# A hybrid recurrence–attention block on eight cores: output projection and first layer norm woven into the next tile's projections, recurrence steps spread, row loads on another queue

## Chip, cores, metric

One Trainium2 chip, all 8 cores; each core works through 2 of the 16 sequences, and no core waits for another. The time of a run is that of the slowest core, in device microseconds (us). A run is *slow* when the four cores of one die are granted a lower TensorE clock than the others and end over 1% later, or when it is over 1.5% above the fastest of the same kernel. Only fast runs are compared, and within a slow run only the cores of the undisturbed die. Engines: PE = TensorE, PEld = its weight loads, DVE = VectorE, ACT = ScalarE, POOL = GpSimd, SP = SyncE.

## The reference, cut

```python
BATCH, SEQ, D_MODEL = 16, 4096, 1024      # D_FF = 2816
def reference(x, c, ...):
    mod = (silu(c) @ w_ada + b_ada)[:, None, :]
    sh1, sc1, g1, sh2, sc2, g2 = jnp.split(mod, 6, axis=-1)
    h = x * (1.0 + sc1) + sh1
    proj = h @ w_in
    aq, af, ai, ag, bq, bk, bv, bf, gates = jnp.split(proj, splits, axis=-1)
    ya = hgrn2_mixer(aq, af, ai, ag, ...)      # gated linear recurrence, 4 heads of 128, head norm, output gate ag
    yb = forgetting_attention(bq, bk, bv, bf)  # causal softmax attention with decay, 8 heads of 64
    gate_a, gate_b = jnp.split(sigmoid(gates), 2, axis=-1)
    merged = gate_a * (ya @ w_branch_a) + gate_b * (yb @ w_branch_b)
    x = layer_norm(ALPHA * x + (1.0 + g1) * (merged @ w_out), ln1_w, ln1_b)
    h = x * (1.0 + sc2) + sh2
    ffn = (silu(h @ w_ffn_gate) * (h @ w_ffn_up)) @ w_ffn_down
    return layer_norm(ALPHA * x + (1.0 + g2) * ffn, ln2_w, ln2_b)
```

## The kernel before

A tile is 512 tokens; a core has 16 of them. The loop over tiles has three stages: M(i) merges the branches of tile i, P(i+1) makes the projections and the recurrence of tile i+1, and F(i) (feed-forward) runs interleaved with A(i+1) (attention). Weights come from HBM in pieces of up to 1 MB through a ring of buffers, all requested on SP's queue in the order of use; `get_piece` waits for the next, `release` frees the oldest.

```python
def load_bc(slot, src, reads=()):                 # one row of norm or gate weights, to all partitions
    P.dma("sync", "bc%d" % slot, bc[:, slot, :], src.partition_broadcast(128), ...)

def ln_acc(s4, nh, b):                            # residual add, half a row block
    TT("vector", TMP[:, ti, :], ps[b], bc[:, 0, ...], mult, ...)
    STT(sl, sl, ALPHA, TMP[:, ti, :], mult, add, ...)
    bn_stats(st[:, s4, nh, :], sl)

def stage_P(i, hooks):                            # hooks: ln_norm(3), 8 transposes to h2T, 4 POOL affines
    # piece f: 4 groups of 8 matmuls -> tanh -> TMP[h]
    # piece i: 4 groups -> G[12+s4], and after each group chain(s4):
    def chain(h):                                 # decay of one head
        ACT(X, TMP[h], Ln); scan(Y <- X) on DVE; ACT(eb[h], Y, Exp); ACT(X, Y, Exp, scale=-1)
        TS("gpsimd", TMP[h] affine); TT("vector", G[4+h] <- TMP[h] * X); CP("vector", ebl[h] <- eb[h])
    # piece k: 4 groups, 2 hooks after each
    # piece q: 4 groups -> G[h] = ps * eb[h]; transposes of G[4+h]
    # piece v: 4 groups -> V1; one hook after each
    cstep(0); cnorm1(0)
    # piece Q: 4 groups; after groups 1, 2, 3: cstep(c), cnorm2(c-1), cnorm1(c)
    cnorm2(3)
    # piece g: 4 groups -> tanh (ACT) -> affine (POOL) -> ya = normed * gate (POOL)

    def cstep(c):                                 # one step of the recurrence
        # 16 matmuls 128x128: output from Sbf and from the chunk; state update
        TT("vector", TMP[3] <- ps[bD] + S); TT("vector", S <- TMP[3] * ebl); CP("scalar", Sbf <- S)

def gen_A(i):                                     # attention; the last row sums are exchanged and inverted at its end
    ...
    while pend: do_pv(*pend.pop(0))
    while ev: run_ev()

def stage_M(i):
    load_xT(i + 1)                                # 3 loads on SP's queue
    for nh in range(2):
        # gate a (4 groups of 8), branch a (4 of 4), branch b (4 of 4)
        if nh == 0:
            load_gate(i, 0); load_bc(1, lnv_d[0])             # rows; then x rows on POOL's queue
        # gate b: 4 groups -> tanh, STT, TT -> G[4*nh + dl]
    wos = [get_piece(), get_piece()]
    for s4 in range(4):                           # output projection: one block of 64 matmuls
        for nh in range(2):
            mmt8(b, wos[nh], lhs=G[0:8]); ln_acc(s4, nh, b)
        ln_rstd(s4)
        conv_hT(i + 1, 2 * s4); conv_hT(i + 1, 2 * s4 + 1)    # next tile's input: even ones on DVE, odd ones on ACT
        if s4 > 0: ln_norm(s4 - 1)
    release(2); load_bc(0, lnv_d[1])
```

Of the kernel before, what the change touches and what calls it, by code (L numbers as in the profile page):

```python
# [162 lines left out]
def build(NSEQ, SEQ):  # L163
    NT = SEQ // 512
    NKT = SEQ // 128
    NTI = NSEQ * NT
# [56 lines left out]
    bc = sb("bc", [128, 2, D], F32)  # L223
    rl = sb("rl", [128, 512], F32)
# [134 lines left out]
    def pieces_P():  # L359
        for j in (0, 2, 5, 1, 6, 4, 3):  # L360
            pieces.append((win_s[j], 4096, "win%d" % j))

    def pieces_M():
        for nh in range(2):
            pieces.append((win_s[7 + nh], 4096, "win%d" % (7 + nh)))
            pieces.append((wa_s[nh], 2048, "wa%d" % nh))
            pieces.append((wb_s[nh], 2048, "wb%d" % nh))
            pieces.append((win_s[9 + nh], 4096, "win%d" % (9 + nh)))
        for nh in range(2):
            pieces.append((wo_s[nh], 4096, "wo%d" % nh))  # L370
# [8 lines left out]
    pieces_P()  # L379
    for i in range(NTI):  # L380
        pieces_M()
        if i + 1 < NTI:
            pieces_P()
        pieces_F()
# [30 lines left out]
    for j in (0, 2, 5, 1, 6, 4, 3):  # L415
        conv_win(j)
# [77 lines left out]
    def conv_hT(i, kc):  # L494
        s = i // NT
        sc, sh = modT[:, s, 8 + kc:9 + kc], modT[:, s, kc:kc + 1]
        if kc % 2:
# [13 lines left out]
    def ln_acc(s4, nh, b):  # L511
        sl = xres[:, s4, nh * 512:(nh + 1) * 512]
        ti = (2 * s4 + nh) % 6
# [20 lines left out]
    def load_bc(slot, src, reads=()):  # L534
        P.dma("sync", "bc%d" % slot, bc[:, slot, :], src.partition_broadcast(128), reads=list(reads), writes=["bc%d" % slot])
# [6 lines left out]
    def stage_P(i, hooks):  # L542
# [3 lines left out]
        hooks = list(hooks)  # L546

        def hook(n=1):
            for _ in range(n):
                if hooks:  # L550
                    hooks.pop(0)()

        if t == 0:
            MSET("gpsimd", v2(S[:]), 0.0, ["S"])
            MSET("gpsimd", v2(Sbf[:]), 0.0, ["Sbf"])
            MSET("vector", CT[:, 0, :, :].rearrange("p a b -> p (a b)"), 0.0, ["CT"])

        XY = [(TMP[:, 4, :], TMP[:, 5, :], [Tk(4)], [Tk(5)]), (rl[:], cpO[:], ["rl0", "rl1", "rl2", "rl3"], ["cpOa", "cpOb"])]

        def chain(h):  # L560
            X, Y, XK, YK = XY[h % 2]
# [8 lines left out]


# [6 lines left out]
        release()  # L578
# [8 lines left out]
        release()  # L587

        pvr, pkey = get_piece()
        pv = v3(pvr, 8)  # L590
        for hp in range(4):
            b = rotD()
            mm8(b, pv, pkey, hp, HT, HTK)
            CP("scalar" if hp % 2 else "vector", KT[:, hp, tok0:tok0 + 512], ps[b][:, :], pk(b), ["KT%d_%d" % (t, hp)])
            hook(2)
# [13 lines left out]
        def s2(h):  # L609
            bb = (0, 1, 2, 3)[h]  # L610
# [6 lines left out]
        for h in range(4):  # L617
            b = rotD()
            mm8(b, pv, pkey, h, HT, HTK)
            TT("vector", G[:, h, :], ps[b][:, :], eb[h], ALU.mult, pk(b) + EBK[h], [Gk(h)])  # L620
            if h == 1:
# [5 lines left out]
        def cstep(c):  # L627
# [3 lines left out]
            for h in range(4):  # L631
                hs = slice(h * 128, (h + 1) * 128)
                MM(ps[bO][:, hs], Sbf[:, h, :], G[:, h, cs], True, False, ["Sbf", Gk(h)], pk(bO))
                MM(ps[bO][:, hs], G[:, 12 + c, hs], G[:, 16 + h, cs], False, True, [Gk(12 + c), Gk(16 + h)], pk(bO))
            for h in range(4):
                hs = slice(h * 128, (h + 1) * 128)
                MM(ps[bD][:, hs], G[:, 8 + h, cs], G[:, 12 + c, hs], True, True, [Gk(8 + h), Gk(12 + c)], pk(bD))
# [3 lines left out]
            CP("scalar", v2(Sbf[:]), v2(S[:]), ["S"], ["Sbf"])  # L641

        SQ = [(TMP[:, 4, :], [Tk(4)]), (TMP[:, 5, :], [Tk(5)]), (rl[:], ["rl0", "rl1", "rl2", "rl3"]), (cpO[:], ["cpOa", "cpOb"])]

        def cnorm1(c):
            sq, sqk = SQ[c]
            ACT(sq, ps[3 + c % 2][:, :], AF.Square, pk(3 + c % 2), sqk)

        def cnorm2(c):
            sq, sqk = SQ[c]  # L650
            bR = 2
# [3 lines left out]
            TT("vector", TMP[:, c, :], ps[3 + c % 2][:, :], sq, ALU.mult, pk(3 + c % 2) + sqk, [Tk(c)])  # L655
# [4 lines left out]
        for s4 in range(4):  # L660
# [4 lines left out]
            hook(1)  # L665
# [11 lines left out]
        cnorm1(0)  # L677
# [3 lines left out]
        for hp in range(4):  # L681
            b = rotD()
            mm8(b, pv, pkey, hp, HT, HTK)
            if hp % 2:
                ACT(Q[:, hp, :], ps[b][:, :], AF.Identity, pk(b), ["Q%d" % hp], scale=0.125)
            else:
                TS("vector", Q[:, hp, :], ps[b][:, :], 0.125, None, ALU.mult, None, pk(b), ["Q%d" % hp])
            if hp == 0:
# [10 lines left out]
            else:  # L699
                cstep(hp)  # L700
                cnorm2(hp - 1)
                cnorm1(hp)
            hook(1)
        release()
        cnorm2(3)
# [3 lines left out]
        for h in range(4):  # L709
            b = rotD()  # L710
            mm8(b, pv, pkey, h, HT, HTK)
            ACT(eb[h], ps[b][:, :], AF.Tanh, pk(b), EBK[h], scale=0.5)
            TS("gpsimd", eb[h], eb[h], nwT[:, h:h + 1], nwT[:, h:h + 1], ALU.mult, ALU.add, EBK[h] + ["nwT"], EBK[h])
            TT("gpsimd", ya[:, h, :].rearrange("p (a b) -> p a b", a=4), TMP[:, 0:4, h * 128:(h + 1) * 128],
               eb[h].rearrange("p (a b) -> p a b", a=4), ALU.mult, [Tk(0), Tk(1), Tk(2), Tk(3)] + EBK[h], ["ya%d" % h])
            hook(1)
        release()
        hook(len(hooks))
# [93 lines left out]
    def gen_F(i):  # L812
        for j in range(6):
# [4 lines left out]
            for fl in range(nfl):  # L818
                fc = 4 * j + fl
                ti = fc % 6  # L820
# [47 lines left out]
    def stage_M(i):  # L868
# [3 lines left out]
        for nh in range(2):  # L872
# [17 lines left out]
            pb_r, pb_k = get_piece()  # L890
            pb = v3(pb_r[:, 0:2048], 4)
            b2 = []
            for dl in range(4):
                b = rotM()
# [170 lines left out]
```

## Time and profile before

| | before |
|---|---|
| runs | 6266.2, 6285.6 (fast), 6594.1 (slow) |
| profiled run, cores | 6226.6 to 6265.6 us, clock 0.903 to 0.906 |
| PE busy, slowest core (core 1) | 4955.7 us of 6265.6 |
| one boundary: first gate matmul of M to first feed-forward matmul, mean of tiles 1 to 14, core 1 | 184.1 us, 52.1 idle |
| the 15 feed-forward-and-attention stages together | 2650.7 us, 72.7 idle |

The boundary between tiles is the place to look, as nine tenths of the idle time of the middle tiles lie there (14 x 52.1 = 730 us against 72.7). The prediction shows the lines.

### The profile page before, as it was taken

Reading aid. Unit: us, or ns where it says so; the run is one execution under the profiler, and the core shown is the slowest. Engines: PE = TensorE matmul, PEld = TensorE weight load, DVE = VectorE, ACT = ScalarE, POOL = GpSimd, SP = SyncE. Lnnn points to the kernel's source line nnn. Section 1 sums busy time; section 2 is a strip of 40 time slices with the busy share of each in tenths; the row PEclk is TensorE's granted clock in tenths of the full one; section 3 lists DMA queues with packets and bytes.
Section 4 is the critical chain, followed back from the end, with each engine's and each line's share of the span. In section 5 each row is a group of like instructions: output and inputs, shape, how many; then the busy total and the mean of one; then the engine's idle time right before and its main releaser. Section 6 shows DMA issues by size and latency. Waiting matters only on the chain.

```text
span 6265.6 us, 82655 instructions; the slowest of 8 cores (6226.6 to 6265.6 us)
## 1 busy us (share of the span) xinstructions
PE 4955.7 (79%) x26204; PEld 2019.3 (32%) x26204; DVE 2278.0 (36%) x3257; ACT 2396.2 (38%) x4034; POOL 1460.7 (23%) x1664
## 2 busy tenths in 40 slices
PE   3045796979889797987978687887979798897987
PEld 1011333323333333333333233333333333333333
DVE  0010434343434434334343434344443434334243
ACT  1011232424345363644722232433436263562741
POOL 0011213232222212222122323232231222213122
PEclk7577998989999898999989898999989899998998
DMA  8753334242423334242243425242332424224233
GB/s 169 106 91 104 128 110 157 103 163 90 165 94 120 125 103 150 84 147 91 90 150 110 163 91 176 96 167 87 133 125 103 156 91 157 87 96 140 89 140 108
DMA packets 231940, 759.90 MB, mean 121 GB/s; under 512 B 20017, under 2 KB 110685, under 8 KB 176223
## 3 DMA queue, kind: packets, MB, share of 16 engines
q1 hardware_dynamic: 165922, 637.66, 29.8%
q0 software_dynamic: 53312, 100.17, 6.8%
q10 hardware_dynamic: 12288, 16.79, 1.0%
q8 instruction: 226, 3.70, 0.2%
q14 instruction: 192, 1.57, 0.1%
HBM read 737.25 MB, written 66.60 MB: 128 GB/s over the span
## 4 chain that ended last, share of the span: by engine, by line
PE 59%; issue 10%; DVE 10%; POOL 7%; DMA 7%; ACT 5%; ACTq 1%; DVEq 0%; SPq 0%; POOLq 0%
PE ps L263 58%; POOL xres L277 4%; DMA ring<-win_s 3%; ACT TMP L274 2%; DVE TMP L277 2%; DMA rl<-cpL 2%; DVE rl L755 1%; DVE xres L286 1%; PE ps L266 1%; POOL ya L277 1%; DMA xres<-w_ada 1%; DVE st L516 1%; DVE TMP L286 1%; DVE S L277 1%; ACT PT L274 1%
## 5 line engine op out<-in xcount | busy, mean ns | idle before, releaser
L263 PE MATMUL ps<-hT,ring 128*128 128x512 bf16 x4608 | 1160.3, 411 | 599.1 <-DVE G L292 261.0
L274 ACT ACTIVATE PT<-ps,nb 128x512 bf16<-128x512 f32 (+3 forms) x2304 | 1311.5, 654 | 650.6 <-PE ps L263 644.1
L263 PE MATMUL ps<-h2T,ring 128*128 128x512 bf16 x5632 | 1320.1, 384 | 67.4 <-DVE TMP L286 60.7
L274 ACT ACTIVATE TMP<-ps 128x512 f32<-128x512 f32 (+1 forms) x760 | 445.5, 591 | 1416.5 <-PE ps L263 1361.3
L286 DVE SCALAR_TENSOR_TENSOR TMP<-TMP,ps 128x512 f32<-128x512 f32 x608 | 414.4, 686 | 1506.3 <-ACT TMP L274 1416.7
L263 PE MATMUL ps<-ring,G 128*128 128x512 bf16 x3840 | 878.5, 382 | 45.2 <-DVE G L277 40.0
L263 PEld LDWEIGHTS ps<-hT,ring 128*128 128x128 bf16 x4608 | 477.3, 105 | 1242.2 <-issue 816.0
L263 PEld LDWEIGHTS ps<-h2T,ring 128*128 128x128 bf16 x5632 | 514.5, 98 | 769.4 <-issue 231.9
L277 POOL TENSOR_TENSOR xres<-xres,bc 128x1024 f32<-128x1024 f32 x256 | 618.3, 2423 | 395.9 <-PE ps L266 369.3
L263 PEld LDWEIGHTS ps<-ring,G 128*128 128x128 bf16 x3840 | 359.5, 98 | 506.8 <-issue 108.4
L277 POOL TENSOR_TENSOR PT<-PT,Ub 128x128 bf16<-128x128 bf16 x512 | 210.1, 428 | 1319.1 <-ACT PT L274 1310.9
L274 ACT ACTIVATE xres<-xres,nmr,rstd 128x1024 f32<-128x1024 f32 x128 | 158.9, 1241 | 583.9 <-POOL nmr L283 537.3
L263 PE MATMUL ps<-PT,V 128*64 128x512 bf16 (+3 forms) x2304 | 344.0, 378 | 19.2 <-ACT cpO L290 17.7
L277 DVE TENSOR_TENSOR G<-TMP,ps 128x512 bf16<-128x512 f32 x352 | 241.7, 687 | 288.9 <-PE ps L263 276.3
L277 DVE TENSOR_TENSOR TMP<-ps,bc 128x512 f32<-128x512 f32 x256 | 174.5, 682 | 470.8 <-PE ps L263 470.8
L263 PE MATMUL ps<-Q,KT 64*128 64x512 bf16 (+3 forms) x2304 | 338.8, 367 | 3.7 <-ACT PT L274 1.9
L755 DVE RECIPROCAL rl<-rl 128x128 f32<-128x128 f32 x256 | 243.0, 949 | 231.1 <-POOL rl L277 213.6
L277 DVE TENSOR_TENSOR G<-TMP 128x512 bf16<-128x512 f32 x160 | 195.2, 1220 | 285.4 <-POOL TMP L283 230.0
L263 PE MATMUL ps<-ya,ring 128*128 128x512 bf16 x512 | 143.8, 437 | 115.5 <-DVE TMP L277 115.5
L522 POOL TENSOR_SCALAR rstd<-mv 128x1 f32<-128x1 f32 x128 | 35.6, 278 | 854.3 <-DVE mv L519 854.3
L263 PE MATMUL ps<-ring,hT 128*128 128x512 bf16 x1024 | 234.1, 379 | 0.0
L263 PE MATMUL ps<-PT,onesb 128*32 128x512 bf16 (+3 forms) x2304 | 224.8, 376 | 0.0
(132 smaller groups left out, 3541.8 us busy)
## 6 DMA issues: line engine op xcount, KB each, us to landing
ring<-win_s SPq DMA_DIRECT2D x176, 1024.0 KB, 6.1
ring<-wg_s SPq DMA_DIRECT2D x80, 1024.0 KB, 4.9
ring<-wu_s SPq DMA_DIRECT2D x80, 1024.0 KB, 4.9
ring<-wd_s SPq DMA_DIRECT2D x64, 1024.0 KB, 5.0
xres<-x POOLq DMA_DIRECT2D x64, 512.0 KB, 16.6
ring<-wo_s SPq DMA_DIRECT2D x32, 1024.0 KB, 16.9
y<-xres POOLq DMA_DIRECT2D x64, 512.0 KB, 3.7
xres<-w_ada SPq DMA_DIRECT2D x24, 1024.0 KB, 7.1
```

Source lines behind the costliest of these rows:

```text
L263: P.op("tensor", lambda e: e.matmul(out, lhsT=lhsT, rhs=rhs, start=start, stop=stop), r, w)
L266: P.op("tensor", lambda e: e.transpose(out=out, in_=in_, identity=ident), r, w)
L274: P.op("scalar", lambda e: e.activation(out=out, in_=in_, func=func, **kw), r, w)
L277: P.op(eng, lambda e: e.tensor_tensor(out=out, in0=in0, in1=in1, op=op), r, w)
L286: P.op("vector", lambda e: e.scalar_tensor_tensor(out=out, in0=in0, scalar=scalar, in1=in1, op0=op0, op1=op1), r, w)
L516: P.op("vector", lambda e: e.bn_stats(out=st[:, s4, nh, :], in_=sl), ["xres%d" % s4], ["st%d_%d" % (s4, nh)])
L522: P.op("gpsimd", lambda e: e.tensor_scalar(out=r1, in0=mv[:, s4, 1:2], scalar1=LN_EPS, scalar2=None, op0=ALU.add), ["mv%d" % s4], ["rstd%d ...
L755: P.op("vector", lambda e: e.reciprocal(out=a, in_=a), RLK, RLK)
```

## The change

Its intent: keep PE fed across the boundary. The output projection and the first layer norm of tile i are cut into 8 groups and hung between the groups of P(i+1); the output gate g goes first in P and k last but one; the four recurrence steps are spread over K and Q; the row loads move from SP's queue to POOL's. `AG` is a new buffer, so that g can be kept until the norms. Core of the diff:

```diff
-    def pieces_P():
-        for j in (0, 2, 5, 1, 6, 4, 3):
+    def pieces_P(wo):
+        seq = [(win_s[j], 4096, "win%d" % j) for j in (3, 0, 2, 1, 6, 5, 4)]
+        if wo:
+            seq = [(wo_s[nh], 4096, "wo%d" % nh) for nh in range(2)] + seq
 ...
-        if kc % 2:
+        if kc % 2 or kc == 2:                      # conv_hT: five of eight on ACT
             ACT(hT[:, kc, :], ...)
 ...
     def load_bc(slot, src, reads=()):
-        P.dma("sync", "bc%d" % slot, ...)
+        P.dma("gpsimd", "bc%d" % slot, ...)
 ...
+    def wo_groups(i):                              # 8 closures: one group of 8 matmuls + ln_acc (+ ln_rstd, ln_norm)
+        ...
-    def stage_P(i, hooks):
+    def stage_P(i, prev):
+        hook(wog, 2)
+        # piece g first: 4 groups -> tanh -> POOL affine -> AG[h], hook(wog) after each
+        # piece f: 4 groups, hook(wog) after the first two (the list is then empty)
+        hook(norm3)                                # ln_norm(3), ahead of the chains
         # piece i with the four chains
-        # piece k with 2 hooks a group
-        # piece q ; piece v with a hook a group
+        # piece q, then piece v: hook(trs), one transpose block, after each group
         cstep(0)
-        cnorm1(0)
-        # piece Q: cstep, cnorm2, cnorm1 after groups 1, 2, 3 ; piece g
+        # piece k: hook(affs) after each group; cnorm(0), cstep(1) after group 1
+        cnorm(1); cstep(2)
+        # piece Q: cnorm(2), cstep(3) after group 1
+        cnorm(3)
 ...
     def cstep(c):
-        # output matmuls, then state matmuls
+        # state matmuls, then output matmuls
         CP("scalar", v2(Sbf[:]), v2(S[:]), ["S"], ["Sbf"])
+        sq, sqk = SQ[c % 2]
+        ACT(sq, ps[bO][:, :], AF.Square, pk(bO), sqk)
 ...
     # stage_M: gate b now before branch b; the output projection leaves M
+            if nh == 1 and i + 1 < NTI:
+                for kc in range(8):
+                    conv_hT(i + 1, kc)
-        wos = [get_piece(), get_piece()]
-        for s4 in range(4): ...
```

## The prediction

> **What bounds the kernel now.** Each of the 8 cores works through 16 tiles of 512 tokens, one after the other. A tile has a "merge" stage M (branch gates, branch outputs, output projection, first layer norm), then the next tile's "projection" stage P (seven 1 MB weight pieces and the recurrence), then a stage in which the feed-forward of the tile is interleaved with the attention of the next. I read the page first, then all of TensorE's waits, then the order of time around one boundary between tiles.
>
> ```profile
> PE 4955.7 (79%) x26204; PEld 2019.3 (32%) x26204; DVE 2278.0 (36%) x3257; ACT 2396.2 (38%) x4034; POOL 1460.7 (23%) x1664
> PE   3045796979889797987978687887979798897987
> PEclk7577998989999898999989898999989899998998
> ```
>
> No engine but PE (TensorE) is near full, and PE dips once per tile. The list of PE's waits (total us, times, longest) names the dips:
>
> ```profile
> PE ps L263 <- DVE G L292: 261.0, 17, 231.0
> PE ps L263 <- DMA ring<-win_s: 196.3, 17, 15.1
> PE ps L263 <- DVE TMP L277: 188.1, 49, 10.5
> PE ps L266 <- ACT xres L274: 140.9, 16, 9.4
> PE ps L263 <- DVE hT L283: 126.6, 14, 9.3
> ...
> PE ps L263 <- DVE TMP L286: 62.4, 55, 3.9
> PE ps L263 <- DVE G L277: 53.8, 33, 5.2
> PE ps L263 <- ACT cpO L274: 53.7, 16, 3.4
> ```
>
> The 231 us is one wait at start-up; the others come about 14 to 16 times, once a tile. I cut PE's timeline at the first gate matmul of M and the first feed-forward matmul. From one to the other it takes 179 to 188 us for tiles 1 to 14, mean 184, with 48 to 58 us idle, mean 52; the feed-forward and attention stage takes 141 to 214 us (it grows with the position) and idles only 2 to 12. So M and P are bound by waits, the other stage by work, and a gain must come from the 52. Idle time costs a second time: after a gap PE issues 512-column matmuls 0.43 us apart instead of 0.216. Counting a boundary's matmuls at the fast rate, 480 x 0.2157 = 103.5 us plus 14 for transposes, recurrence and norms gives 118; elapsed less idle is 132. So about 14 us a boundary are cold matmuls and small gaps. The boundary at 2754 to 2935 us, in order of time (start, duration, engine, what, wait before it):
>
> ```profile
> 2797.58 0.32 SPq L119 DMA_DIRECT2D bc<-modrow  x1
> 2798.00 0.37 SPq L119 DMA_DIRECT2D bc<-ln1w  x1
> 2798.06 0.59 POOL L119 DMA_DIRECT2D y<-xres  x1 [0.56 <-POOL xres L277]
> 2798.53 0.32 SPq L119 DMA_DIRECT2D ring<-win_s  x1
> ...
> 2810.54 1.86 PE L263 MATMUL ps<-hT,ring 128*128 128x512 bf16 x4 [11.25 <-DMA ring<-win_s]
> ```
>
> The row load `bc<-modrow` overwrites a buffer that POOL still reads for the previous tile's last layer norm. It waits on the same in-order queue as the weights, so the gate piece behind it goes out only at 2798.5 and PE waits 11.25 us.
>
> **What the Trainium skill says.** "TensorE: Matmul & The Clock Gate", Part 1 (the HAM clock gate), has the PE clock halved after an idle window of about 3.4 us until it has been busy for about as long. The trace agrees: after the 11.25 us gap the weight loads are 0.43 us apart, and the clock records hold only 0.5 and 1.0. So gaps over some 3.4 us carry roughly 2 us extra each. "DMA: Bandwidth & Descriptors", section "Issuing engines are not separate DMA queues": queues share 16 engines, so moving the row loads buys no bandwidth. What it can buy here is that the weights need not stand behind a waiting row load. "GPSIMD Engine Reference", key points: POOL shares its SBUF interface with VectorE. The trace agrees: the state update S takes DVE 0.69 us alone and 2.0 to 2.1 while POOL runs the affine steps.
>
> **The change, part by part.** No matmul is added or removed; only orders, queues and buffers move.
>
> (1) Row loads leave the weight queue, and the branch-b gate now goes before the branch-b product. The gate piece is then requested when its ring place comes free. Wait of 180.6 us over tiles 1 to 15: about 11.3 us a tile off the path.
>
> (2) The output projection (64 matmuls, 14 us) is no longer a block. Today it waits 2.5 us for G, and the next tile's hT conversion is queued behind its norm work on DVE and ACT, so P starts with 9.3 us of wait. In the new order hT is converted before the branch-b product and the 8 projection groups alternate with 8 groups of P. DVE needs 3 x 0.69 = 2.1 us plus gaps per group against 3.5 us of PE per pair: it keeps up. But G is later: after the last gate DVE does three conversions (1.6 us) and then four pairs of 0.69 + 0.69 plus gaps (6.3), together 7.9, while PE has 3.6 us of branch product. A wait of about 4.3 us remains. Net: 11.8 out, 4.3 in.
>
> (3) Today the fourth row group's normalisation sits in ACT's queue behind the four decay chains, and the first h2T transpose waits 9.1 us for it. It moves ahead of the chains: gone. But the K piece, which stood between the chains and q, moves behind them. The chains are serial, 2857.6 to 2873.3 us in this boundary, about 3.8 us a head. I laid PE's i and q groups over those times, with three PSUM banks for the projections: waits of 1.8 (there already), 0.8, 2.6 and 2.0 us. Today this part has 1.8 + 9.1 = 10.9; then about 7.2.
>
> (4) The recurrence steps today stand in three places of Q with waits of 3.9, 0.8 and 3.4 us around them (plus 0.5 at the first). Spread over K and Q, with two groups (3.5 us) of matmul between step and next step, and with the squares' reduction after them, I allow 0.5 + 1.2 + 1.0. The POOL affines still overlap there, so the S update will often stay at 2 us.
>
> (5) The output gate g of the recurrence is computed first, not last. Today POOL's eight operations (0.77 and 1.27 us, four of each) end after P does, and hold the feed-forward's buffers:
>
> ```profile
> 2939.93 1.26 POOL L277 TENSOR_TENSOR ya<-TMP,PT 128x512 bf16<-128x512 f32 x1
> 2941.28 0.60 ACT L274 ACTIVATE TMP<-ps 128x512 f32<-128x512 f32 x1 [1.93 <-POOL ya L277]
> 2941.78 3.77 ACT L274 ACTIVATE PT<-ps,nb 128x512 bf16<-128x512 f32 x6
> 2941.98 0.69 DVE L286 SCALAR_TENSOR_TENSOR TMP<-TMP,ps 128x512 f32<-128x512 f32 x1 [12.64 <-ACT TMP L274]
> 2942.78 0.56 PEld L263 LDWEIGHTS ps<-h2T,ring 128*128 128x128 bf16 x4 [2.44 <-issue]
> 2942.81 1.02 PE L263 MATMUL ps<-h2T,ring 128*128 128x512 bf16 x4 [1.98 <-DVE TMP L286]
> ```
>
> The feed-forward also starts at another temporary, so these 2.0 to 3.1 us (mean about 2.4, outside the 52) go.
>
> What stays: the wait of the branch-a product at the start of M (7.7 us a tile on average, 6.8 here), which is the attention's last row-sum exchange and reciprocal on DVE, and the 1.0 to 1.5 us after it for ACT. Their order is unchanged.
>
> Sum per boundary: idle afterwards 8.7 (start of M) + 4.3 (G) + 7.2 (chains) + 2.7 (steps) + 1 (rest) = 24, against 52: 28 off. Feed-forward start: 2.4. Cold and small gaps: 14 now; three gaps over 3.4 us at 2 us each leave about 6.5: 7.5 off. Together 38 us, so a boundary of about 148 instead of 184 (and 2 in the stage behind). Fifteen such boundaries: 15 x 38 = 570. The last tile gains only the weight wait and its cold start, about 12. The first P gains some 10 (its waits in the steps, 2.0, 1.9 and 3.4, and g's 7 us done before POOL is free of its start-up DMA issues). In all 590. From the two fast runs of before, 6266 and 6286, mean 6276: 5686. I take off less, 560, since every remaining wait that I have overlooked adds and none subtracts: **5715 us**.
>
> **Rivals.** (a) The weight wait only changes its name, to bandwidth. For: in the 10 us windows around 2804 to 2824 the DMA engines are 100% busy at 355 and 411 GB/s, and the new M packs weights, x, y, xT and rows (about 16 MB) into 55 us, some 300 GB/s. Against: most of that time weights are requested one to two pieces ahead. If it holds, 4 to 6 us a tile come back: about 5790. (b) DVE becomes the bound in P, since projections' drains, ln work and chains are now packed closer, with POOL's affines slowing it. DVE is busy 84 of 181 us in this boundary; in 146 it would be 58%, so not on average, but in places. It would cost 5 to 8 us a boundary: about 5820. (c) The x rows come late: they are issued at 2798 to 2810 and take 16.6 us (median), while the first norm step would now run near 2812. PE has five banks for the projection and four g groups in between, 12 to 16 us of cover; I expect no loss, at worst 4 us a tile: 5775. (d) The waits hide each other more than I laid out, chains and G below my estimate: about 5620. (e) A denser PE is clocked lower or the slow state is more frequent: the slow run of before (6594) shows that there is one, but the long feed-forward stages, 98% clock at 95% PE, show no reduction in a fast run.
>
> **Range and chances.** (a) and (b) together give the upper end, 5850; (d) the lower, 5610. 2% is 126 us, not a quarter of the expected gain; even parts (1) and (5) alone give 14 x 15 = 210. Faster 0.97, same 0.02, slower 0.01.
>
> **What would show it.** The wait on the `win_s` ring falls from 196 to under 60 us, most of that at start-up; those for hT and for ACT's xres vanish; a wait of the output projection for G of about 4 us a tile appears; waits on DVE's casts and products of 1 to 3 us sit in i and q; the wait at the branch-a product stays near 115 us over the run; half-clock time falls from 1218 us to below 900. PE's busy share rises to about 85%. The prediction is wrong if boundaries stay above 165 us, if ring waits stay above 5 us a tile, or if the feed-forward stage gets longer.

## The result, and the profile after

| us | before | after |
|---|---|---|
| fast runs | 6266.2, 6285.6 | 5769.6, 5775.2, 5789.0 |
| slow runs | 6594.1; 6719.3 (run beside the changed kernel) | 6038.6 |
| ratio of fast runs | | 0.921, 95% interval 0.916 to 0.926 |
| the same in a later session (run *after_again* below) | 6271.5 to 6288.0 | 5748.8 to 5781.4; ratio 0.918 (0.915 to 0.921) |

A ratio here is the mean time of one kernel's fast runs over that of the other's of the same rounds, so not quite the ratio of the medians. The median over all four runs of the changed kernel is 5782 us. The time lies in the predicted range, 55 to 75 us above the predicted point.

The page of the changed kernel's slowest core (core 7), the lines that answer to the first three of the prediction:

```profile
PE 4927.4 (85%) x26204; PEld 2017.0 (35%) x26204; DVE 2270.8 (39%) x3245; ACT 2407.0 (42%) x4050; POOL 1505.4 (26%) x1756
PE   4036788998999898999988898989999998998987
PEclk7567899999999999999999999999989898999988
```

PE's slices are 8 or 9 almost throughout after the start-up, where before many fell to 7 or 6, and its count of instructions is the same. The list of PE's waits on core 1, an undisturbed core (total us, times, longest us):

```profile
PE ps L264 <- DVE G L293: 273.9, 32, 216.3
PE ps L264 <- DVE TMP L278: 119.5, 17, 9.8
...
PE ps L264 <- DVE G L278: 93.3, 34, 5.2
PE ps L264 <- ACT rl L275: 64.9, 31, 2.6
...
PE ps L264 <- ACT cpO L275: 31.7, 16, 2.4
...
PE ps L264 <- DMA ring<-win_s: 11.3, 2, 9.0
...
PE ps L267 <- ACT xres L275: 6.0, 3, 2.1
```

Against the list of before: the wait for weights (`ring`) fell from 196.3 to 11.3 us, that for ACT's `xres` from 140.9 to 6.0, that for `hT` (126.6) has left the list. The waits that grew are those for DVE's casts of `G` (the decay chains), from 261.0 − 231.0 = 30 to 273.9 − 216.3 = 58 us, and for DVE's products `G` (output projection and chains), from 53.8 to 93.3. Of the squares of the recurrence, `rl` is new with 65 us, and `cpO` fell from 54 to 32. The wait for `TMP` at the start of M stayed.

I cut the timeline of PE into the same parts on three cores. All numbers are us; the last column is the slowest core of the later session's profiled run, where no clock but 0.5 and 1.0 was recorded.

| part | predicted difference | before, core 1 | after, core 1 | after_again, core 4 |
|---|---|---|---|---|
| until the first projection matmul | 0 | 124 | 127 | 130 |
| start-up boundary (P(0), A(0), M(0), P(1)) | −46 | 667.3 | 626.1 | 639.1 |
| boundaries of tiles 1 to 14 | 14 x −36 | 2577.5 (184.1 each) | 2086.1 (149.0) | 2108.3 (150.6) |
| 15 feed-forward-and-attention stages | −36 | 2650.7 | 2636.3 | 2638.5 |
| last tile's M to its feed-forward | −12 | 96.6 | 92.4 | 98.6 |
| the rest | 0 | 149.5 | 154.5 | 155.0 |
| span | −598, of which some 30 held back | 6265.6 | 5722.4 | 5769.6 |

Core 1 was the slowest of its run before and the fastest after, so its two columns flatter the change. Means over all cores whose clock shows no 0.8125 (see below):

| us | before, 8 cores | after, 6 cores | after_again, 8 cores |
|---|---|---|---|
| boundary of tiles 1 to 14 | 182.9 | 149.4 | 149.7 |
| 15 feed-forward-and-attention stages | 2649.7 | 2636.8 | 2636.8 |
| span | 6243.5 | 5731.1 | 5748.4 |

So the boundary reached the level that was worked out (predicted 148 with 24 idle; measured 149.0 with 24.7 on core 1), but the mean gain was 33.5 us and not 36; the rest of what is missing sits elsewhere. Three places can be seen in the trace. First, the recurrence steps. The order of time around one of them on core 1 (start, duration, engine, what, wait before it):

```profile
2657.93 0.69 DVE L278 TENSOR_TENSOR S<-TMP,ebl 128x512 f32<-128x512 f32 x1
2658.77 0.62 ACT L291 CAST Sbf<-S 128x512 bf16<-128x512 f32 x1 [4.28 <-DVE S L278]
2659.29 0.59 ACT L275 ACTIVATE rl<-ps 128x512 f32<-128x512 f32 x1
2660.03 1.10 PE L264 MATMUL ps<-rl,onesf 128*128 128x512 f32 x2 [2.65 <-ACT rl L275]
```

ACT stood idle for 4.28 us in front of the copy of the state, which needs DVE's update; the square, which needs nothing but PSUM, stands behind it in ACT's queue, and PE waits 2.65 us for it. Second, the start of the feed-forward:

```profile
2684.38 2.41 ACT L275 ACTIVATE PT<-ps,nb 128x512 bf16<-128x512 f32 x4
2686.80 1.28 ACT L275 ACT_TABLE_LOAD   x1
2688.10 0.60 ACT L275 ACTIVATE TMP<-ps 128x512 f32<-128x512 f32 x1
2688.80 0.69 DVE L287 SCALAR_TENSOR_TENSOR TMP<-TMP,ps 128x512 f32<-128x512 f32 x1 [3.46 <-ACT TMP L275]
2689.63 1.02 PE L264 MATMUL ps<-h2T,ring 128*128 128x512 bf16 x4 [1.36 <-DVE TMP L287]
```

The wait for POOL is gone. Four exps stood ahead of the first tanh before, too; new between them is a reload of ACT's function table of 1.28 us. Before, the reload lay in the last groups of P, in time in which ACT had been idle, because g's tanhs came last:

```profile
2930.44 1.28 ACT L274 ACT_TABLE_LOAD   x1 [1.97 <-PE ps L263]
```

Now g comes first and the norms' exps last. It is so in all 15 stages: the reload starts 3.8 to 5.0 us after the first feed-forward matmul, where before it started 4.9 to 5.3 us ahead of it. PE's waits in the first 8 us of a stage fell only from 2.5 to 1.8 us (core 1, mean of 15). The Trainium skill, "ScalarE: Activation LUTs", section "What ACT_TABLE_LOAD costs", has some 1283 ns for the load, and the trace agrees; of the drain of 1380 ns that it adds, the trace shows nothing: the tanh starts 0.02 us after the load ends. Third, the last tile: its M shrank from 65.2 to 50.4 us, but from the output projection to the feed-forward it then took 42.0 instead of 31.4 us, because nothing is woven between the groups there and the norm is exposed.

The cores differed too. The profiled run, core by core (span, mean granted clock):

```profile
core 1: 5722.4 us, clock 0.934
...
core 6: 5778.8 us, clock 0.917
core 7: 5787.5 us, clock 0.918
```

Cores 6 and 7 carry 469 and 476 us of clock records at 0.8125, in three stretches of some 160 us, most of each in M and P and 20 to 27 us in the feed-forward; the six others carry none.

### The profile page after: what moved, and what is told of

The parts are those of the page before. It is cut to its first block, busy times and chain, and to the rows that moved or that the text cites. A ratio compares the mean times of both kernels' runs of the same rounds, so it can differ in the third digit from the quotient of the medians.

```text
span 5787.5 us, 82483 instructions; the slowest of 8 cores (5722.4 to 5787.5 us)
## 1 busy us (share of the span) xinstructions
PE 4927.4 (85%) x26204; PEld 2017.0 (35%) x26204; DVE 2270.8 (39%) x3245; ACT 2407.0 (42%) x4050; POOL 1505.4 (26%) x1756
## 3 DMA queue, kind: packets, MB, share of 16 engines
q1 hardware_dynamic: 152098, 587.32, 29.9%
## 4 chain that ended last, share of the span: by engine, by line
PE 70%; issue 10%; DVE 7%; ACT 5%; DMA 5%; POOL 2%; ACTq 1%; DVEq 0%; POOLq 0%; SPq 0%
PE ps L264 69%; DMA rl<-cpL 2%; DVE rl L794 1%; DVE S L278 1%; PE ps L267 1%; ACT TMP L275 1%; ACT PT L275 1%; DMA xres<-w_ada 1%; ACT rl L275 1%; DMA ring<-win_s 1%; DVE TMP L278 1%; DVE TMP L287 1%; POOL xres L278 1%; ACTq L119 1%; DMA ring<-wd_s 1%
## 5 line engine op out<-in xcount | busy, mean ns | idle before, releaser
L264 PE MATMUL ps<-hT,ring 128*128 128x512 bf16 x4608 | 1117.5, 397 | 337.2 <-DVE G L293 278.7
L264 PE MATMUL ps<-ring,G 128*128 128x512 bf16 x3840 | 922.5, 391 | 69.8 <-DVE G L278 60.0
L287 DVE SCALAR_TENSOR_TENSOR TMP<-TMP,ps 128x512 f32<-128x512 f32 x544 | 367.5, 685 | 1075.6 <-ACT TMP L275 964.2
L264 PEld LDWEIGHTS ps<-hT,ring 128*128 128x128 bf16 x4608 | 459.7, 102 | 919.4 <-issue 512.1
L275 ACT ACTIVATE TMP<-ps 128x512 f32<-128x512 f32 (+1 forms) x632 | 367.3, 590 | 908.2 <-PE ps L264 866.8
L264 PE MATMUL ps<-PT,V 128*64 128x512 bf16 (+3 forms) x2304 | 342.7, 377 | 19.4 <-ACT cpO L291 17.9
L275 ACT ACTIVATE AG<-ps 128x512 f32<-128x512 f32 x128 | 76.5, 597 | 389.7 <-PE ps L264 383.9
L278 POOL TENSOR_TENSOR rl<-rl,cpL 128x512 f32<-128x512 f32 x64 | 81.0, 1265 | 568.7 <-DMA rl<-cpL 426.0
```

The source lines that it names most:

```text
L264: P.op("tensor", lambda e: e.matmul(out, lhsT=lhsT, rhs=rhs, start=start, stop=stop), r, w)
L275: P.op("scalar", lambda e: e.activation(out=out, in_=in_, func=func, **kw), r, w)
L278: P.op(eng, lambda e: e.tensor_tensor(out=out, in0=in0, in1=in1, op=op), r, w)
L287: P.op("vector", lambda e: e.scalar_tensor_tensor(out=out, in0=in0, scalar=scalar, in1=in1, op0=op0, op1=op1), r, w)
```

## The experiments

Sixteen runs were made (after_again and combo_again repeat a kernel), in four sessions on three chips, the kernel before beside each (rows_only to k_cover on one chip, sq_first to recip_last and wo_later on a second, the others on a third, in two sessions). "Boundary" is the mean of tiles 1 to 14 on one core without records at 0.8125, but for two rows: affs_late has the mean of its six such cores; wo_later has no such core, and the mean is over the 92 of its 112 boundaries that no such record touches. The cores of one run differ by 0.5 to 2.3 us, so differences under 1 us say little.

| run | boundary (idle), us | fast runs, us | ratio to before (95%) |
|---|---|---|---|
| kernel before | 184.1 (52.1) | 6260 to 6288 in all sessions | 1 |
| rows_only | 176.5 (45.9) | 6166 to 6208 | 0.987 (0.982–0.991) |
| rows_back | 167.2 (40.6) | 6001 to 6045 | 0.961 (0.956–0.966) |
| wo_block | 158.3 (29.9) | 5891, 5898 | 0.941 (0.939–0.944) |
| k_cover | 158.2 (32.3) | 5900 to 5981 | 0.949 (0.933–0.964) |
| wo_later | 153.4 (27.8) | 5827, 5855 | 0.933 (0.927–0.938) |
| changed kernel, after_again | 149.0, 149.7 (24.7) | 5749 to 5789 | 0.921, 0.918 |
| zero_h (wrong result) | 149.2 (25.1) | 5752 to 5759 | 0.917 (0.915–0.920) |
| conv_act | 148.6 (25.2) | 5742, 5749 | 0.916 (0.913–0.918) |
| affs_late | 146.3 (22.1) | 5708, 5761 | 0.916 (0.906–0.926) |
| recip_last | 146.2 (22.2) | 5693 to 5697 | 0.909 (0.907–0.911) |
| chain3 | 144.0 (19.8) | 5664 | no interval |
| sq_first | 143.8 (20.5) | 5681 to 5718 | 0.909 (0.905–0.912) |
| combo_dve | 133.7 (13.4) | 5515, 5515 | no interval |
| combo, combo_again | 132.5 (11.2) | 5493 to 5500 | 0.875 (0.873–0.877) |
| combo_affs | 132.0 (10.8) | 5472, 5474 | 0.872 (0.869–0.874) |

### Which part of the change carries the gain

**rows_only**: the kernel before with one line changed.

```diff
-        P.dma("sync", "bc%d" % slot, ...)
+        P.dma("gpsimd", "bc%d" % slot, ...)
```

> The kernel before with one change: the row loads go on POOL's queue instead of the weight queue. My theory: the wait of PE for the ring of win_s (11 to 12 us a tile, 196 us in all) goes, and with it about 2 us a tile of cold matmuls; 16 tiles x 13 = about 200 us faster, 6070 in a fast run (ratio 0.965 to 0.97). Rival (bandwidth): the x, y and row transfers still fill the DMA engines there, the wait only shrinks to 5 us or so: ratio about 0.985.

Measured: 0.987, much less than expected, and near the rival's 0.985; but the rival's reason, a ring wait of 5 us a tile that stays, did not come. The waits of PE (core 0) tell where it went:

```profile
PE ps L263 <- DVE G L292: 246.7, 17, 218.2
PE ps L263 <- DVE hT L283: 196.6, 14, 16.1
...
PE ps L263 <- DMA ring<-win_s: 12.7, 1, 12.7
```

On core 0 before, these were 163.4 us for weights and 126.8 for `hT`. The first all but left, the second grew by 70: PE reaches the next tile's projection earlier, and the conversion of its input, queued behind the norm work, is not ready earlier. Nearly half of the freed time turned into that wait, and the boundary fell by 7.6 us (7.0 against the same core's 183.5), not by 11.

**rows_back**: the changed kernel with that one line undone.

> The changed kernel with only the row loads put back on the weight queue. My theory: the ring waits come back, 10 to 12 us a tile at the second gate piece, plus cold matmuls; about 180 us slower than the changed kernel, ratio to before about 0.95. Rival: in the changed order the gate and product of branch b are swapped and the output projection is later, so the weights have slack and the queue hardly matters: ratio stays below 0.93.

Measured: 0.961, boundary 167.2; the weights' wait is back (core 3):

```profile
PE ps L264 <- DMA ring<-win_s: 251.9, 18, 17.9
```

The row loads alone are worth 7.6 us a boundary, all the rest without them 16.9, both together 35.1 (means over the cores: 6.7, 16.8 and 33.5). The parts are not a sum: a removed wait uncovers another.

**wo_block**: the changed kernel with the output projection as one block at the head of P.

```diff
-        hook(wog, 2)
+        hook(wog, 8)
 ...
-        held = 1 if wog else 0
+        held = 0
```

> The changed kernel with all eight output projection groups in one block at the start of P instead of woven in (the hT conversion stays early). My theory: the weave itself matters because the x rows land 10 us after the projection starts and DVE needs 2.2 us a group against 1.7 of PE; with only five banks PE stops in the block: 8 to 12 us a tile more, ratio about 0.945. Rival: what counted was only the early hT conversion, the weave is for nothing: within 1 us a tile, ratio 0.92 to 0.923.

Measured: boundary 158.3, 9.3 us more, as expected. A wait of 100.3 us for ACT's `AG` stands among PE's waits, which the changed kernel does not have: g's tanhs queue behind the norm work that the block brings all at once. The weave itself is worth 9 us a boundary.

**k_cover**: the changed kernel with k back between the chains and q, as before the change, and all steps in Q, one after each group.

```diff
-    (3, 0, 2, 1, 6, 5, 4)
+    (3, 0, 2, 5, 1, 6, 4)
     # piece k moved ahead of q; in piece Q: after group 0 the forget-gate sums, after groups 1-3 cnorm(hp-1), cstep(hp)
```

> The changed kernel with K back between the decay chains and q, the four recurrence steps then in Q alone (one per group). My theory: the 5 us a tile of waits behind the chains shrink to about 2, but the waits around the steps grow from 6 to about 10 and more matmuls run cold; about the same or up to 2 us a tile slower, ratio 0.92 to 0.93. Rival: moving K is what gained most of the step waits, 6 us a tile slower, ratio above 0.935.

Measured: boundary 158.2. Waits of PE (core 4):

```profile
PE ps L264 <- ACT cpO L275: 132.9, 32, 5.3
...
PE ps L264 <- ACT rl L275: 36.4, 16, 3.2
PE ps L264 <- DVE KT L293: 33.1, 16, 2.1
```

The step waits grew from 65 + 32 to 169 us. The wait for the chains' products went (22 to 0 us over the fourteen boundaries), but that for their casts grew (52 to 67), and the casts of k brought a new one of 33: the waits behind the chains did not shrink, and the rival was right in kind, with 8 to 9 us a tile instead of its 6. Moving k behind the chains, as the change does, is what lets the steps be spread.

**wo_later**: the first two groups of the output projection held back until g's second group is out.

```diff
-        hook(wog, 2)
 ...
-            hook(wog)
+            if h:
+                hook(wog, 2 if h == 1 else 1)
```

> The changed kernel with the first two groups of the output projection moved behind the second group of g, so that PE has work while DVE finishes G. My theory: the wait for G (62 us over the run, 3.9 a tile) goes down to under 1 us a tile, and the 10 or so cold matmuls after it too: 5 us a tile, 60 to 80 us faster than the changed kernel, ratio about 0.909. Rival: hT is not converted early enough on ACT, the wait only changes its name to hT: ratio about 0.92.

Measured: 0.933, slower than the changed kernel; both theories missed. Part of that time is clock: all eight cores of the profiled run carry 283 to 453 us at 0.8125. Without those boundaries it still loses about 4 us a boundary. The wait for `G` at the output projection fell to 3.4 us over the run, as meant, but the two `wo` pieces are held longer in the ring, and the wait for weights rose from 11.3 to 78.1 us (13 times, longest 10.5); half-clock time rose from 753 to 809 us. A ring place is a resource of the weave too.

### The terms that were mis-sized

**sq_first**: in the recurrence step, the square ahead of the state's copy on ACT.

```diff
-            CP("scalar", v2(Sbf[:]), v2(S[:]), ["S"], ["Sbf"])
             ACT(sq, ps[bO][:, :], AF.Square, pk(bO), sqk)
+            CP("scalar", v2(Sbf[:]), v2(S[:]), ["S"], ["Sbf"])
```

> The changed kernel, in each recurrence step ACT takes the square of the output before the copy of the state, not after. The prediction allowed 2.7 us a tile for waits around the steps, the trace shows 5.8, and the reduction of the squares waits for ACT, whose queue has the state copy (it waits for DVE's state update) ahead of the square. If that order is the cause, the waits on rl and cpO fall by 3 us or more a tile: 40 to 60 us faster than the changed kernel, ratio about 0.912. Rival (the step itself is what PE waits for, as the state copy feeds the next step a moment later): the wait only moves to the state copy, within 10 us, ratio about 0.92.

Measured: as expected; boundary 143.8. The waits for the squares `rl` and `cpO` (97 us) are gone from the list, and this one is there instead:

```profile
PE ps L264 <- ACT Sbf L291: 17.8, 17, 1.1
```

The state's update is no shorter here, so it was the order on ACT that put the update in PE's way.

**affs_late**: POOL's affines after the last norm, out of the way of DVE's state updates.

```diff
-            hook(affs)          # after each group of k
```

> The changed kernel, POOL's eight affine steps not between the groups of K but after the last norm of P[...]. If the slowed state update (2.1 us instead of 0.7) is what the step waits come from, they fall by 2 to 3 us a tile: 30 to 45 us faster, ratio about 0.914. Rival (order in ACT's queue, see the square): no more than 10 us, and the affines then slow the start of the feed-forward.

Measured: boundary 146.0 to 146.6 on cores 2 to 7 (cores 0 and 1 carry 160 us at 0.8125), 3.1 us less than the changed kernel's mean of 149.4, at the upper end of the expected gain; the ratio's interval is too wide to add anything. The waits for `rl` and `cpO` fell from 65 + 32 to 29.2 + 26.2 us (core 1), but stayed: with ACT's order as it was, a shorter update takes away not quite half of the step waits; sq_first takes away all but 18 us.

**recip_last**: the last exchange of row sums and the last reciprocals of the attention are held back until the feed-forward beside it has been issued (the number is a weight in the interleaving of the two).

```diff
         while pend:
             do_pv(*pend.pop(0))
+        yield 600
         while ev:
             run_ev()
```

> The changed kernel, with the attention's last row-sum exchange and its reciprocals put behind the last norm step of the feed-forward in the order of DVE. The wait at the branch-a product in M (117 us over the run) was foreseen as staying: its bank is held by that norm step, which stands behind the reciprocals, which wait for a transfer. If so it goes, and a wait for yb of 2 to 3 us a tile takes its place: 6 to 8 us a tile with the cold matmuls, 90 to 120 us faster than the changed kernel, ratio about 0.903. Rival: the product of branch a then waits as long for ACT or for yb: ratio above 0.915.

Measured: 0.909, boundary 146.2. The wait at the start of M, 119.5 us in the changed kernel, is down to 4.0, but a ring wait came up:

```profile
PE ps L264 <- DMA ring<-win_s: 88.4, 16, 10.9
```

The last row block of the next tile's input is loaded into `rl` on SP's queue, and has to wait until DVE is done with `rl`; the weights stand 0.5 us behind it. The late reciprocals did not cause this: in the changed kernel, too, that load goes out 16 to 20 us after the start of M (mean 17.8 us, here 17.9). PE had stood at the branch-a product meanwhile, and only now comes early enough to need the weights. It is the fault of the kernel before once more, with another buffer, and one removed wait uncovers another.

**chain3**: two decay chains in flight, with a third pair of buffers.

```diff
-        def chain(h):
+        def chain1(h):             # Ln, scan
+        ...
+        def chain2(h):             # two exps, affine, product
 ...
-            chain(s4)
+            chain1(s4)
+            if s4 > 0:
+                chain2(s4 - 1)
+        chain2(3)
```

> One part alone: in the projection of v the four decay chains are software-pipelined. The front half of chain h+1 (Ln on ACT, scan on DVE) is issued before the back half of chain h (two exps on ACT, the affine on POOL, the product on DVE), with a third pair of buffers in the unused slices 8 to 11 of PT; nothing else moves. Theory: in the changed kernel the first matmul of k and the two transposes of q wait for G because DVE and ACT run each chain end to end, in lockstep, and every chain costs two round trips between the two engines; with two chains in flight the round trips hide, the waits for DVE G at the chains fall from about 5 us a tile to 1 to 2, and the span falls by some 75 us: ratio to the kernel before 0.905 to 0.912 (changed kernel 0.921), boundary mean 144 to 146 us (149 now). Rival: ACT's own work bounds this stretch (tanhs, conversions of the hidden tile, exps), so the order of the halves moves nothing: chain waits stay at 4 to 6 us a tile and the ratio at 0.917 to 0.925.

Measured: one fast run, 5664.4 us; divided by the mean of the fast runs of the kernel before in the same session, 6273.7, that is 0.903, without an interval, as four of its five runs were slow. The undisturbed dies of those four end at 5655 to 5662 us too. Boundary 144.0. The wait for DVE's casts after the chains, 52 us over the fourteen boundaries, is down to 0.2; that for the products stayed (22). The theory held.

**conv_act**: the conversions that DVE still made (three of eight, and not four as the expectations here and at combo_dve say), on ACT, but for the first tile.

```diff
-        if kc % 2 or kc == 2:
+        if i > 0 or kc % 2:
```

> One part alone: the four conversions of the hidden tile that DVE still made (of eight) are made by ACT for every tile but the first; nothing else moves. Theory: the wait for G at the end of the woven output projection (4 us a tile) is DVE being late with the x rows, the residual adds and the conversions that stand between them; without the conversions the wait falls to about 2.5 us a tile, with fewer matmuls at half clock behind it, and the span falls by 25 to 45 us: ratio 0.913 to 0.917, boundary mean 146 to 147.5. Rival: ACT is then the one that is late: a wait for hT written by ACT appears at the first gate matmuls (2 us a tile or more), and the ratio is 0.920 to 0.93.

Measured: the ratio, 0.916, is in the expected interval, yet the theory fell: the boundary is 148.6 against 149.0 to 150.6 of the changed kernel's cores, and the wait for `G` at the output projection fell only from 3.9 to 3.4 us a tile, with no wait on ACT. The ratio looks like a gain only beside the 0.921 of the first result; beside the changed kernel on the same chip (0.918, 0.915 to 0.921) it is none that the intervals can tell apart.

### The clock

**zero_h**: scale and shift of the hidden tile's conversion set to 0. The result is wrong.

```diff
-            ACT(hT[:, kc, :], ..., scale=sc, bias=sh)
+            ACT(hT[:, kc, :], ..., scale=0.0, bias=0.0)
```

> A wrong result on purpose: the changed kernel with the scale and the shift of the hidden tile's conversion set to 0, so that the moving operand of all projections is zero; same instructions, same waits, same transfers. It asks what makes pairs of cores drop to a clock of 0.8125 for stretches of some 160 us in the changed kernel's projection stages (never seen in a fast run of the kernel before). Theory: the throttle answers to the power that the data draws: no record of 0.8125 on any core outside a slow die, all cores within 0.5% of each other near 5720 to 5740 us, and no or fewer slow runs among the five. Rival: the throttle answers to how many matmuls are issued, whatever they carry: pairs of cores at a mean clock of 0.91 to 0.92 with 20 to 60 us more span, and slow runs as often as in the changed kernel.

Measured: no core of a fast run with a clock below 0.931, fast runs at 5752 to 5759; but four of its seven runs were slow, and the fast runs of the other kernels of the session show no pairs of slower cores either. So nothing follows about the data, and the chip had to be asked with the changed kernel itself.

**after_again**: no edit; the changed kernel on the chip of zero_h.

> The changed kernel once more, unaltered. Theory: the stretches at 0.8125 belong to chip and hour, not to the change: if this chip shows none in the four-kernel job before, the fast runs take 5735 to 5757 us, with all cores within 5715 to 5757 and mean clocks of 0.931 to 0.937, ratio 0.914 to 0.917. Rival: they belong to the denser weave of the changed kernel's projections (the kernels of the earlier job each altered that weave or its data): fast runs at 5765 to 5790 with pairs of cores at 0.915 to 0.926, ratio 0.919 to 0.923.

Measured: fast runs at 5748.8, 5753.4, 5769.7, 5771.1 and 5781.4, and in the profiled one no record at 0.8125 on any core. The theory is right that the stretches do not belong to the change, but its times miss: without them the kernel is hardly faster. Traces of the other sessions say the same of the stretches: rows_only, the kernel before but for one line, carries 349 to 486 us at 0.8125 on cores 4 to 7 of a fast run, on two of them more in the feed-forward stages than in M and P; k_cover, sq_first and affs_late carry them on two cores each, wo_later on all eight, and the profiled fast runs of the third chip on none. The profiled run's slowest core:

```profile
core 4: 5769.6 us, clock 0.928
```

It spent 837 us at half clock, against 749 to 783 us on the other seven. So cores differ in gaps and half clock, with or without those stretches; why this one has more of it is open. My explanation of the miss by the 13/16 clock fell.

### A version that beats both

**combo**: sq_first, recip_last, chain3 and conv_act together, and the eighth row block of the input on POOL's queue:

```diff
-        P.dma("sync", "xT2", rl[:], src[:, 7, :], writes=xsk(7))
+        P.dma("gpsimd" if i else "sync", "xT3" if i else "xT2", rl[:], src[:, 7, :], writes=xsk(7))
```

> A version meant to beat both kernels: the changed kernel with the square ahead of the state copy in the recurrence step (measured alone: boundary 143.8 us against 149), the last denominators of the attention flushed after the feed-forward's weights are under way (alone: boundary 146.2), the pipelined decay chains and the conversions on ACT (both beside this run), and the eighth hidden row block loaded on POOL's queue, so that it does not hold up weights on SP's. If the four gains add (5.2 + 2.8 + 4 + 2 us a tile, fifteen tiles, plus the ring wait of 71 us that the late flush had made), the span is 5480 to 5560 us, ratio 0.87 to 0.885, boundary mean 134 to 138. Rival: they share waits, as ACT sits in all of them: boundary 139 to 142, 5570 to 5640 us, ratio 0.89 to 0.90.

Measured: 5500.3 us (one fast run of six), boundary 132.5, below the expected 134 to 138. The four gains alone are 5.2 + 2.8 + 5.0 + 0.4 = 13.4 us a boundary; together, with the row block moved, they are 16.5. The ring wait is down to 12.9 us, as the weights no longer stand behind that row block.

**combo_again**: no edit, for an interval.

> The combined version once more, unaltered, for an interval: 5490 to 5510 us in the fast runs, ratio 0.875 to 0.879; if pairs of cores fall to 0.8125, up to 5550 and 0.885.

Measured: 0.875 (0.873–0.877), fast runs at 5492.8 to 5499.7.

**combo_dve**: combo without the line of conv_act.

> The combined version without one part: four of the eight conversions back on DVE. Alone, moving them gained nothing (boundary 148.6 against 149.0). Theory: in the combined version what ends last at the woven output projection is DVE (the wait for G has grown from 4.1 to 6.9 us a tile there, as the wait for the attention's ya is gone), so the conversions, 4 x 0.7 us of DVE's time in that stretch, now do lie on the path: without the part the wait for G grows to 8.5 to 10 us a tile and the boundary from 132.5 to 135 to 136, span 5530 to 5550, ratio 0.881 to 0.885. Rival: as when alone, nothing moves: 5490 to 5510.

Measured: 5515.4 and 5515.5 us, boundary 133.7. The wait for DVE's `G` (core 1), of which 125.5 us belong to the output projection in the fourteen boundaries, 9.0 a tile against 7.2 in combo:

```profile
PE ps L264 <- DVE G L278: 161.4, 34, 11.0
```

So the theory is right in kind and the gain smaller than I put it: what gained 0.4 us alone gains 1.2 a boundary (1.5 in the means over all cores) once the waits in front of it are gone.

**combo_affs**: combo and affs_late.

> The combined version, and POOL's affines of the first layer norm all after the last recurrence step, so that DVE's state updates are not stretched by POOL (2.0 us instead of 0.69 where they overlap). Alone it gained 2 us a tile, through the waits for the square that the combined version no longer has. Theory: in the combined version the state update is off the path but for the 1 us a tile that PE waits for the state's copy, so it gains 0 to 1 us a tile: 5485 to 5510. Rival: the shorter updates free DVE for what follows and it gains 2 us again: 5460 to 5475; or the affines arrive late for the feed-forward and it loses: over 5520.

Measured: 0.872 (0.869–0.874), 5471.9 and 5473.9 us, 5% below the changed kernel in the same session (mean 5764.9). PE's waits (core 5, of the undisturbed die, as the profiled run was slow):

```profile
PE ps L267 <- DVE ebl L293: 220.5, 1, 220.5
PE ps L264 <- DVE G L278: 147.3, 34, 10.8
PE ps L264 <- DMA xres<-w_ada: 114.4, 14, 32.5
```

The first and third lie in the start-up; the wait for `Sbf` (17 us) is gone. In the boundary only the wait for `G` is still large. The theory of 0 to 1 us a boundary held (131.2 to 132.0 on cores 4 to 7, against 131.7 to 133.1 in combo), but the fast runs lie below its 5485 to 5510 and in the interval of the first rival, 5460 to 5475: which of the two is right stays open.

## Why the prediction was right or wrong

Two steps failed: the waits around the recurrence steps, term (4), were mis-sized, and the gain at the start of the feed-forward, term (5), mostly did not come. The numbers of one core were taken for all.

- **What bounds the kernel: right.** On core 1, PE's idle in the boundary fell from 52.1 to 24.7 us (predicted 24), the boundary to 149.0 (148), half-clock time from 1218 to about 760 us (below 900), PE's share to 85%.
- **(1) Row loads, −11.3 us a tile: the total came out, the term did not.** The wait for weights left (196.3 to 11.3 us), but as one part it is worth 7.6 us if done alone (rows_only) and 18.2 if done last (rows_back). Adding the waits up as if each were independent gave the right sum only because the change removes all of them. (The prediction's 180.6 us over fifteen tiles are 12.0 a tile, not 11.3; its sum starts from the idle time that stays and does not use this figure.)
- **(2) Output projection: right; the wait at the start of M stayed too (7.8 us, predicted 7.7).** Wait for `G` 3.9 us a tile, predicted 4.3; the weave is worth 9.3 (wo_block). The cause, DVE late at the end of M, was shown only in combo_dve.
- **(3) Chains, 7.2 us after: right in kind, 5.3 measured.** The four waits around one boundary were 2.05, 0.64, 1.98 and 1.63 us against 1.8, 0.8, 2.6 and 2.0.
- **(4) Recurrence steps, 2.7 us after: this term failed; 6.2 measured** (59.3 + 27.7 us over the fourteen boundaries). I had laid out PE and DVE and left out that ACT takes its work in order: the square behind the copy of the state. sq_first shows it. Term 3 was 1.9 us too high and term 4 3.5 too low; that the idle time still came out near 24 is in part luck.
- **(5) Feed-forward start, −2.4 us a tile: this step failed.** POOL's wait did go, but the wait at the start fell only from 2.5 to 1.8 us, and the stages gained 14.4 us instead of 36. The same reordering that freed POOL put the norms' exps at the end of P, and with them a reload of ACT's table in front of the first tanh. I had asked what the tanh waited for before, and not what would stand in front of it after. No run took the reload away alone, so its share of the missing 22 us is read from the trace and not shown by experiment; 15 x 1.28 = 19 us is an estimate of it.
- **Last tile, −12 predicted: −4 on core 1, +2 on core 4 of after_again. Start-up, −46: −41 and −28.** The last tile has nothing to weave with, so the new order exposes its norm.
- **The span.** The terms sum to −598 (the prediction, with 2 for 2.4 us, wrote −590). Measured: −543 between the two profiled core 1s, −512 between the means of the cores, −496 from core 1 before to the slowest core of after_again. What is missing from −598 is, on core 1, 22 us of term 5, 13 of the fourteen boundaries, 8 of the last tile, 5 of the start-up and 8 at the two ends; the held-back 30 us covered half of it. On core 4 of after_again another 22 are missing at the boundaries (150.6 against 149.0 us) and 13 at the start-up, with ring waits no larger than 18 us in all. These are differences between cores, which I did not put in: every term was read from core 1, the slowest before, and taken for all eight.
- **Rivals.** (a), bandwidth, did not come: 11.3 us of ring wait. (b), DVE as the bound in P, did not come as such. (c), late x rows, did not stop PE in woven tiles. (d), hidden waits, appeared as the opposite: waits hid *behind* each other, so that parts alone gained less. (e) I dismissed because the feed-forward stages ran at full clock; the 0.8125 stretches of the first result lie mostly in M and P, so the argument looked in the wrong place. They are not needed for the miss, as after_again shows, and what causes them stays open.

## What to carry to other kernels

Waits in a row cover each other: judge a part by taking it out of the finished whole as well as by doing it alone, and do not expect the two numbers to agree. When you move work, follow every in-order queue it passes through, DMA issue and ACT included, and ask what now stands in front of the first instruction that the critical engine needs; a load or a copy that waits for its buffer holds up everything behind it. Here one line, the queue of the row loads, was worth 18.2 us a boundary when done last, and the order of two instructions on ACT 5.2, against 9.3 for the whole weave. And read a gain on all cores: the slowest core before need not be the slowest after.

## What the Trainium skill lacked or had wrong

- "DMA: Bandwidth & Descriptors", section "Issuing engines are not separate DMA queues", says that issuing on several engines saves only the time to initiate a DMA. The section does not speak of a DMA that waits for its buffer and holds up those behind it in its engine's order, nor of what that costs. Row loads back on SP's queue: 251.9 us of waits for weights instead of 11.3, boundary 167.2 instead of 149.0 us. One input block on that queue: 88.4 (recip_last) instead of 12.9 us (combo, which differs in other parts too).
- "ScalarE: Activation LUTs", section "What ACT_TABLE_LOAD costs", adds a drain of 1380 ns to each load. Here the load takes 1.28 us, and in 31 of the changed kernel's 33 loads (core 1) it starts 0.02 us after the end of the instruction before it, and the next instruction starts 0.01 us after its end.
- "TensorE: Matmul & The Clock Gate", Part 1, describes a limit to 13/16 of the clock for a whole die when three of its cores run dense matmuls, and has all-core kernels budgeted for it. The slow runs agree with the whole die (conv_act: 2851 to 2904 us at 0.8125 on all of cores 0 to 3). But combo ran fast on all eight cores, PE busy for 87% of the span, with no record at 0.8125, and in the first result cores 6 and 7 had 469 and 476 us of it while 4 and 5 of the same die had none. Whether data decides, as the page says, zero_h leaves open: only its projections were zero, and four of its seven runs were slow.
- "GPSIMD Engine Reference", key points, names the contention of POOL and DVE and gives no size in that place. Here a 128x512 f32 product on DVE took 2.0 us (median of 61) instead of 0.69 while POOL ran. Taking POOL's affines out of its way was worth 3.1 us of a boundary of 149, and under 1 of 132.5 in the combined version.
